# FFN weights split by the transfers that load them, and not by VectorE

## The chip, the cores and the metric

The kernel runs on one core of one Trainium2 chip. The metric is the device time of one execution in microseconds (us); the median of 3 runs of the kernel before is 906.88 us (905.92 to 911.09). A core has TensorE (PE: matrix products, with a row PEld for the loads of the stationary operand), VectorE (DVE), ScalarE (ACT), GpSimd (POOL) and SyncE (SP), each with an instruction stream that it takes in order. Transfers are issued from SP, ACT or POOL, run on 16 DMA engines that all of them share, and report their end through a semaphore.

## The reference

One layer of a decoder trunk is computed for 512 prompt positions and 8 sample rows (520 columns in all): a mixer sub-layer (window attention, a state-space branch "S5" and attention to a memory, gated and merged), and after it a channel sub-layer. Only that second part, the FFN, changes how it is fed:

```
def conv_ffn(h, lp, prev):
    a = h @ lp['w_ffn_gate']          # 1024 x 2816
    up = h @ lp['w_ffn_up']           # 1024 x 2816
    ...
    c = lp['conv_b'] + sum(w[j] * ext[:, j:j + T] for j in range(CONV_W))
    y = (jax.nn.gelu(c) * up) @ lp['w_ffn_down']   # 2816 x 1024
```

Products are wanted in float32 accuracy. TensorE is used in its faster float32r form, so each float32 operand is split into a rounded part "hi" and the rest "lo" = value - hi, and a product is taken as hi*hi + hi*lo + lo*hi: three matrix instructions in place of one.

## The kernel before

All weights lie in one tensor `in_w`, cut into 152 units of up to 8 blocks of 128x128 in the order of use (`UNITS`, line 43). A unit of 8 blocks is a tile of 128 partitions x 1024 float32, 512 KB. The last 68 units are the FFN's: 22 pairs "fg" (gate) and "fu" (up), and then 8 groups of three "dn" (down) units, of which the third has 6 blocks (384 KB). Before them stand 8 units "out" of the mixer's output projection.

Each unit takes three steps. `w_load` (line 323) issues the transfer into one of two raw tiles `wraw` from SP. `w_split` (line 335) has ACT round it into one of three tiles `whi`, and DVE subtract `whi` from `wraw` into one of three tiles `wlo`. Then `product` (line 449) issues the matrix products: 8 blocks x 2 halves of the columns x 3 = 48 instructions of 260 columns. The order is set in the code: `begin` (431) makes sure that unit i is split and units i+1 and i+2 are loaded, and in the middle of unit i `ahead` (441) splits i+1 and i+2 and loads i+3. By the time that `ahead` runs, i+1 is split and i+2 loaded, so what it really issues is the split of i+2 and after it the load of i+3.

In the FFN loop (line 1576) a pair also has, after "fg", DVE reading the result out of PSUM, a small copy on POOL, a convolution on ACT and DVE, an add and two more copies on POOL, a Gelu on ACT, and after "fu" a product, a rounding and a subtraction that make the hidden block's hi and lo. The "dn" loop (1616) has no work on POOL.

Up to the "out" units, smaller tasks (attention, S5, memory) are woven between the matrix products by a planner: `Clock` (line 79) books an estimated cost for every instruction, and `pump` (394) starts the next step of a task when the booked time says that it is ready. A transfer from POOL is booked in line 201 with one figure; the S5 task uses it where it writes a kernel matrix to a scratch tensor `kd` and reads it back (lines 1159 and 1164). In the FFN no such task is left and the planner moves nothing.

Lines 1547 and 1548 copy two caches from input to output (508 KB each) from POOL's queue. All instructions go through one helper, so the profile names line 226 for nearly all of them; tiles tell them apart.

Of the kernel before, what the change touches and what calls it, by code (L numbers as in the profile page):

```python
# [7 lines left out]
F32 = mybir.dt.float32  # L8
F32R = mybir.dt.float32r
I32 = mybir.dt.int32  # L10
AF = mybir.ActivationFunctionType
OP = mybir.AluOpType
# [3 lines left out]
P = 128  # L16
# [5 lines left out]
KB = DM // P  # L22
# [33 lines left out]
def stream_units():  # L56

    u = [("k", 0), ("v", 0)] + [("q", i) for i in range(4)]
    u += [(x[:-1], int(x[-1])) for x in SEQ0.split() if x != "vt"]
    u += [(x[:2], int(x[2])) for x in SEQ.split()]  # L60
    u += [("gB", i) for i in range(8)] + [("glu", i) for i in range(8)]
    u += [("out", i) for i in range(8)]
    for i in range(NFF):
        u += [("fg", i), ("fu", i)]
    for i in range(8):
        u += [("dn", (i, 0)), ("dn", (i, 1)), ("dn", (i, 2))]
    return u


UNITS = stream_units()  # L70


def unit_blocks(u):
    return 6 if u[0] == "dn" and u[1][1] == 2 else 8


UNIT_OFF = []
_o = 0
for _u in UNITS:
    UNIT_OFF.append(_o)  # L80
# [4 lines left out]
class Clock:  # L85
# [74 lines left out]
    def op(self, eng, name, a, k):  # L160
        outs = [a[0]] + ([k["accum_out"]] if "accum_out" in k else [])
        ins = [x for x in list(a[1:]) + list(k.values()) if hasattr(x, "ap") and x is not outs[-1]]
        shape = a[0].shape
        n = 1
        for d in shape[1:]:
            n *= d
        if eng == "sp":
            out, src = a
            n = 4
            for d in out.shape:  # L170
                n *= d
            t0 = max(self.t["sp"], self.deps(eng, [out], [src]))
            self.t["sp"] = t0 + 0.45
            self.t["hw"] = max(self.t["hw"], t0 + SP_A) + max(0.26, n / 360e3)
            self.note(eng, [out], [src], self.t["hw"] + SP_B)
            return
        if eng == "pe":
            if name == "transpose":
                c = 0.9e-3 * a[1].shape[0] + 0.003
            else:  # L180
                m, w = 1, 1
                for d in a[1].shape[1:]:
                    m *= d
                for d in a[2].shape[1:]:
                    w *= d
                c = 0.417e-3 * max(m, w) + 0.003 if a[1].dtype == F32R else 1.667e-3 * w * (1 if m > 64 else 0.5)
        elif eng == "act":
            c = 0.833e-3 * n + 0.094 * (1 + sum(hasattr(k.get(x), "ap") for x in ("bias", "scale", "accum_out")))
            if a[1].space == PSUM:
                c -= 0.043  # L190
        elif eng == "dve":
            if name == "tensor_reduce":
                n = 1
                for d in a[1].shape[1:]:
                    n *= d
            c = 0.07 + (6.3e-3 if name == "reciprocal" else 0.52e-3 if name == "tensor_copy" and a[1].space != PSUM
                        else 1.04e-3) * n
            if name == "tensor_tensor_reduce" or name == "scalar_tensor_tensor" and hasattr(a[2], "ap"):
                c += 0.06
        elif eng == "dma":  # L200
            c = 3.3
        else:
            c = {"tensor_tensor": 0.151 + 1.95e-3 * n, "tensor_scalar": 0.215, "memset": 0.035 + 0.833e-3 * n}.get(name, 0.12 + 3.3e-3 * n)
        q = "pool" if eng == "dma" else eng
        t0 = max(self.t[q], self.deps(eng, outs, ins))
        if eng == "pe" and t0 < COLD:
            c *= 2
        end = t0 + c
        self.t[q] = t0 + 1.1 if eng == "dma" else end
        self.note(eng, outs, ins, end)  # L210
        if eng != "dma":
            self.last = max(self.last, end + self.LAT)
        else:
            self.last_dma = end
# [26 lines left out]
HZ = 2.0  # L241
# [7 lines left out]
N_RAW = 2  # L249
# [7 lines left out]
def body(ctx, tc, I, O):  # L257
    nc = tc.nc
    clk = Clock()
    pe, act, dve, pool = [Eng(r, n, clk) for r, n in ((nc.tensor, "pe"), (nc.scalar, "act"), (nc.vector, "dve"),  # L260
                                                      (nc.gpsimd, "pool"))]
    sp = Eng(nc.sync, "sp", clk)
# [3 lines left out]
    wrw = ctx.enter_context(tc.tile_pool(name="wrw", bufs=N_RAW))  # L266
    wsp = ctx.enter_context(tc.tile_pool(name="wsp", bufs=3))
# [15 lines left out]
    def B_done(n=1):  # L283
        live["B"] -= n
# [36 lines left out]
    RAW, HI, LO = {}, {}, {}  # L321

    def w_load(i, parts=1):
        if i >= len(UNITS) or i in RAW:
            return
        n = unit_blocks(UNITS[i]) * P
        r = clk.tile(wrw.tile([P, KB * P], F32, name="wraw", tag="wraw"), "wraw", N_RAW)
        RAW[i] = r
        m = n // parts
        for c in range(parts):  # L330
            yield sp.dma_start(r[:, c * m:(c + 1) * m],
                               bass.AP(tensor=I["w"].tensor, offset=I["w"].offset + UNIT_OFF[i] + c * m,
                                       ap=[[n, P], [1, m]]))

    def w_split(i, part=None):

        if i >= len(UNITS) or (part is None and i in HI):
            return
        for _ in w_load(i):
            pass  # L340
        n = unit_blocks(UNITS[i]) * P
        if not part:
            HI[i] = clk.tile(wsp.tile([P, KB * P], F32R, name="whi", tag="whi"), "whi", 3)
            LO[i] = clk.tile(wsp.tile([P, KB * P], F32R, name="wlo", tag="wlo"), "wlo", 3)
        c = slice(0, n) if part is None else slice(part * n // 2, (part + 1) * n // 2)
        r = RAW[i]
        act.activation(HI[i][:, c], r[:, c], AF.Copy)
        dve.tensor_tensor(LO[i][:, c], r[:, c], HI[i].bitcast(F32)[:, c], op=OP.subtract)
# [9 lines left out]
    pos = [0]  # L358

    def run(l):  # L360
        clk.last = l.ready if l.eng else 0.0
        cur.append(l)
        try:
            r = next(l.gen)
            l.ready = clk.last
            l.eng, l.need, l.tiles = "pe", 1, 0
            if isinstance(r, tuple):
                r, l.tiles = r
            if isinstance(r, str):
                l.eng, l.need = r, 0  # L370
            elif isinstance(r, float):
                l.ready = max(l.ready, clk.last_dma) + r
            elif r is not None:
                l.need = abs(r)
                if r < 0:
                    l.eng = None
        except StopIteration:
            lanes.remove(l)
        cur.pop()

    ev = [EV]

    def unit_time(i):
        return {"mk": 2.65, "mv": 2.65, "sk": 0.85, "sv": 0.85}.get(UNITS[i][0], 5.3)

    def ready(l):

        if l.eng in ("dve", "act"):
            t = 0.0 if l.ready <= clk.t[l.eng] + MARG_Q else l.ready
        else:  # L390
            t = max(l.ready if l.eng else 0.0, clk.free("SD", 4, l.need))
        return max(t, clk.free("T2", N_T2, l.tiles))

    def pump(rem=0.0):

        while True:
            t = clk.t["pe"]
            lim = min(rem + ev[0], rem + sum(unit_time(j) for j in range(pos[0], min(max(HI) + 1, len(UNITS)))) - HZ)
            if clk.t["dve"] - t > min(BACK_D, lim) or clk.t["act"] - t > min(BACK_A, lim):
                return  # L400
            for l in lanes:
                if ready(l) <= t + MARG:
                    run(l)
                    break
            else:
                return
# [24 lines left out]
    def begin(name):  # L431
        i = pos[0]
        assert UNITS[i][0] == name, (UNITS[i], name)
        pos[0] += 1
        if i:
            w_split(i)
            load(i + 1)
            load(i + 2)
        return i
# [128 lines left out]
    sv = con.tile([P, 528], F32, name="sv")  # L568
    ap = sv[:, 0:288].rearrange("p (n r q) -> p n r q", n=9, r=2)
# [239 lines left out]
    for m in range(1, 4):  # L809
        i = begin("q")  # L810
# [699 lines left out]
    for m in range(8):  # L1510
        i = begin("glu")
# [23 lines left out]
    for m in range(8):  # L1535
        i = begin("out")
# [7 lines left out]
            dve.tensor_tensor(acc2, acc2, sq, op=OP.add)  # L1544


    pool.dma_start(O["sk"][:, :127 * 128], I["ckn"][:, 128:])
    pool.dma_start(O["sv"][:, :127 * 128], I["cvn"][:, 128:])
    B_done(2)
    hb = [B(F32R) for _ in range(5)]  # L1550
    hm = M(F32R)
# [24 lines left out]
    for ob in range(NFF):  # L1576
        i = begin("fg")
        if ob == 0:

            ps = product(i, range(8), blk(yh, yl), kouter=True, mid=norm2)  # L1580
            i = begin("fu")
# [7 lines left out]
        w = [cw[:, ob, j:j + 1] for j in range(3)]  # L1589
        c = T2()  # L1590
# [9 lines left out]
        if ob:  # L1600
            i = begin("fu")
# [14 lines left out]
    for m in range(7):  # L1616
        ps = out_tile()
        for c in range(3):
            i = begin("dn")
            n = unit_blocks(UNITS[i])  # L1620
# [209 lines left out]
```

## Time and profile before

| | |
|---|---|
| median of 3 runs | 906.88 us |
| the profiled execution | 907.0 us |
| its span, first to last instruction | 905.2 us |
| mean granted TensorE clock | 0.987 |
| PE busy | 883.5 us, 98% |
| DVE busy | 518.8 us, 57% |
| ACT busy | 344.8 us, 38% |
| POOL busy | 130.3 us, 14% |
| DMA | 97.83 MB, mean 108 GB/s |

A busy share is that of the whole span. Matrix instructions overlap each other, so the distance between their starts, and not their length, is the time that one of them takes. [...] POOL's own transfers are the profile's "software_dynamic" queue, SP's and ACT's are "hardware_dynamic".

### The profile page before, as it was taken

The page shows a single profiled execution, that of the slowest core. Times are in us where ns is not written, and L with a number is a line of the kernel's source. Part 1 is how long each engine was busy: PE and PEld are TensorE (multiplying, and loading weights), DVE is VectorE, ACT ScalarE, POOL GpSimd, SP SyncE. Part 2 cuts the span into 40 slices and gives each one's busy share as a digit, 9 for nine tenths or more (in the row PEclk, how much of TensorE's full clock was granted, in tenths as well). Part 3 has the DMA queues.
Part 4 walks back from the last instruction along what each step waited for, and adds up shares of the span by engine and source line. Part 5 has one row for each costly group of instructions (what it writes and reads, how often), then busy time and mean ns, then how long its engine had stood idle before and what let it go on. Part 6 is the DMA issues. An engine that isn't in the chain of part 4 may idle for free.

```text
span 905.2 us, 17660 instructions
## 1 busy us (share of the span) xinstructions
PE 883.5 (98%) x7417; PEld 854.0 (94%) x7417; DVE 518.8 (57%) x868; ACT 344.8 (38%) x596; POOL 130.3 (14%) x376
## 2 busy tenths in 40 slices
PE   8999999999899999999999999999999999999994
PEld 8998899998799899899999999999999999999993
DVE  6777768794465696023665665555555555232224
ACT  6376655544434322142333333333333333222231
POOL 7887110002000002100000010000110011000001
PEclk9999999999999999989999999999999999999997
DMA  7533482345424433524232323332222223223212
GB/s 253 171 93 102 128 183 71 117 134 135 89 79 151 120 97 115 137 70 171 91 98 89 103 81 95 93 94 93 94 92 93 88 90 97 94 88 105 89 42 94
DMA packets 38383, 97.83 MB, mean 108 GB/s; under 512 B 12464, under 2 KB 15968, under 8 KB 38032
## 3 DMA queue, kind: packets, MB, share of 16 engines
q1 hardware_dynamic: 35136, 89.53, 32.1%
q0 software_dynamic: 1936, 6.02, 3.0%
q8 instruction: 58, 0.95, 0.4%
q10 hardware_dynamic: 1232, 1.16, 0.4%
q14 instruction: 21, 0.17, 0.1%
HBM read 91.47 MB, written 6.26 MB: 108 GB/s over the span
## 4 chain that ended last, share of the span: by engine, by line
PE 86%; DMA 5%; DVE 4%; ACT 2%; issue 1%; POOL 1%; SPq 0%; DVEq 0%; ACTq 0%; POOLq 0%
PE mm L226 76%; PE SD L226 11%; DMA B<-kd 2%; DMA wraw<-in_w 2%; DVE B L226 1%; ACT T L226 1%; DVE T L226 1%; DMA out_fin<-B 1%; DMA B<-in_xT 1%; DVE wlo L226 1%; DMA kd<-B 1%; ACT whi L226 1%; ACT B L226 0%; POOL B L226 0%; DVE TN L226 0%
## 5 line engine op out<-in xcount | busy, mean ns | idle before, releaser
L226 PE MATMUL mm<-B,whi 128*128 128x260 f32 (+1 forms) x4128 | 761.5, 285 | 4.1 <-DVE B L226 2.4
L226 PEld LDWEIGHTS mm<-B,whi 128*128 128x128 f32 x4128 | 641.9, 189 | 12.4 <-issue 4.1
L226 PE MATMUL mm<-B,wlo 128*128 128x260 f32 (+1 forms) x2096 | 594.1, 283 | 1.1 <-DVE wlo L226 1.0
L226 PEld LDWEIGHTS mm<-B,wlo 128*128 128x128 f32 x2096 | 396.8, 189 | 1.9 <-DVE wlo L226 1.9
L226 DVE TENSOR_TENSOR wlo<-wraw,whi 128x1024 fp32r<-128x1024 f32 (+2 forms) x157 | 186.6, 1190 | 167.8 <-ACT whi L226 167.0
L226 ACT ACTIVATE whi<-wraw 128x1024 fp32r<-128x1024 f32 (+2 forms) x157 | 160.4, 1023 | 113.0 <-PE mm L226 71.2
L226 DVE SCALAR_TENSOR_TENSOR T<-T,sm,T 128x512 f32<-128x512 f32 x44 | 34.0, 772 | 25.8 <-ACT T L226 25.1
L226 ACT ACTIVATE T<-T,sm 128x520 f32<-128x520 f32 x22 | 18.1, 823 | 79.1 <-POOL T L226 79.1
L226 PE MATMUL SD<-B 128*64 128x72 f32 (+9 forms) x576 | 43.5, 248 | 0.8 <-DMA B<-kd 0.7
L226 DVE TENSOR_TENSOR B<-B 128x256 f32<-128x256 f32 (+11 forms) x78 | 36.3, 474 | 13.8 <-ACT B L226 12.4
L226 ACT ACTIVATE B<-T 128x520 fp32r<-128x520 f32 (+1 forms) x32 | 20.4, 638 | 55.0 <-DVE T L226 55.0
L226 POOL COPY T<-T 128x2 f32<-128x2 f32 x22 | 4.1, 184 | 255.1 <-DVE T L226 255.1
L226 PEld LDWEIGHTS SD<-B 128*64 128x64 f32 (+5 forms) x576 | 30.4, 126 | 10.9 <-issue 4.0
L226 ACT ACTIVATE B<-SD 128x256 fp32r<-128x256 f32 (+6 forms) x50 | 19.0, 406 | 53.5 <-PE SD L226 53.4
L226 DVE TENSOR_TENSOR T<-mm,rstd 128x520 f32<-128x520 f32 x22 | 15.4, 699 | 34.2 <-PE mm L226 31.1
L226 ACT ACTIVATE T<-B 128x520 f32<-128x520 f32 (+1 forms) x25 | 15.3, 611 | 39.8 <-DVE B L226 39.8
L226 ACT ACTIVATE T<-T 128x520 f32<-128x520 f32 (+2 forms) x26 | 16.0, 621 | 37.6 <-DVE T L226 35.9
L226 ACT ACTIVATE B<-B,sm 128x520 fp32r<-128x520 f32 (+1 forms) x23 | 16.7, 726 | 30.6 <-DVE B L226 27.3
L226 ACT ACTIVATE B<-mm 128x520 f32<-128x520 f32 x16 | 9.7, 605 | 47.3 <-PE mm L226 47.3
L226 DVE TENSOR_TENSOR B<-T,B 128x520 fp32r<-128x520 f32 (+1 forms) x30 | 19.2, 640 | 12.9 <-ACT B L226 12.7
L226 ACT ACTIVATE T<-T,TN 128x257 f32<-128x257 f32 (+3 forms) x48 | 21.8, 473 | 11.3 <-DVE TN L226 11.3
L226 POOL MEMSET T<- 128x2 f32 (+2 forms) x27 | 4.7, 175 | 147.4 <-DVE B L226 81.5
(156 smaller groups left out, 657.6 us busy)
## 6 DMA issues: line engine op xcount, KB each, us to landing
wraw<-in_w SPq DMA_DIRECT2D x144, 512.0 KB, 3.5
wraw<-in_w SPq DMA_DIRECT2D x8, 384.0 KB, 3.0
B<-in_xT SPq DMA_DIRECT2D x1, 2080.0 KB, 10.6
B<-kd POOLq DMA_DIRECT2D x16, 128.0 KB, 7.0
B<-in_xT SPq DMA_DIRECT2D x4, 260.0 KB, 6.3
B<-in_xT SPq DMA_DIRECT2D x2, 520.0 KB, 8.1
out_y<-B SPq DMA_DIRECT2D x4, 260.0 KB, 3.0
out_y<-B ACTq DMA_DIRECT2D x4, 260.0 KB, 3.2
```

What stands on the lines that cost most here:

```text
L226: return g(*a, **k)
```

## The change

For the FFN's 68 units the raw load from SP is gone. `w_load` issues a transfer from POOL whose destination is float32r, so that it writes the rounded hi part itself; the tiles used are five, two that were `wraw` and three `whi`. `w_split` has ACT write -hi into the `wlo` tile, and then POOL issues a second transfer of the same weights that adds them onto it: w + (-hi) = lo. DVE's subtraction is gone for these units, and each unit is read from memory twice. The planner books a POOL transfer at 5.0 in place of 3.3, and the two cache copies are issued from SP.

```diff
+FFN0 = UNITS.index(("fg", 0))
...
         elif eng == "dma":
-            c = 3.3
+            c = 5.0
...
     def w_load(i, parts=1):
         if i >= len(UNITS) or i in RAW:
             return
+        if i >= FFN0:
+
+            n = unit_blocks(UNITS[i]) * P
+            t = (clk.tile(wrw.tile([P, KB * P], F32R, name="wraw", tag="wraw"), "wraw", N_RAW) if i % 5 < 2 else
+                 clk.tile(wsp.tile([P, KB * P], F32R, name="whi", tag="whi"), "whi", 3))
+            RAW[i] = HI[i] = t
+            yield pool.dma_start(t[:, :n], w_dram(i))
+            return
...
+    def w_dram(i):
+        n = unit_blocks(UNITS[i]) * P
+        return bass.AP(tensor=I["w"].tensor, offset=I["w"].offset + UNIT_OFF[i], ap=[[n, P], [1, n]])
+
     def w_split(i, part=None):
 
-        if i >= len(UNITS) or (part is None and i in HI):
+        if i >= len(UNITS) or (part is None and i in LO):
             return
         for _ in w_load(i):
             pass
+        if i >= FFN0:
+
+            n = unit_blocks(UNITS[i]) * P
+            LO[i] = clk.tile(wsp.tile([P, KB * P], F32R, name="wlo", tag="wlo"), "wlo", 3)
+            act.activation(LO[i][:, :n], HI[i].bitcast(F32)[:, :n], AF.Copy, scale=-1.0)
+            pool.dma_start(LO[i][:, :n], w_dram(i), accum_op=OP.add)
+            return
...
-            lim = min(rem + ev[0], rem + sum(unit_time(j) for j in range(pos[0], min(max(HI) + 1, len(UNITS)))) - HZ)
+            lim = min(rem + ev[0], rem + sum(unit_time(j) for j in range(pos[0], min(max(LO) + 1, len(UNITS)))) - HZ)
...
-    pool.dma_start(O["sk"][:, :127 * 128], I["ckn"][:, 128:])
-    pool.dma_start(O["sv"][:, :127 * 128], I["cvn"][:, 128:])
+    sp.dma_start(O["sk"][:, :127 * 128], I["ckn"][:, 128:])
+    sp.dma_start(O["sv"][:, :127 * 128], I["cvn"][:, 128:])
```

How the instructions stand then is shown at three places. The first is POOL's stream in the middle of the FFN. T2 tiles are a pair's convolution tiles, M holds its small results. Before, POOL has only the small work of one pair after the other:

```order
L226 MEMSET T2_6650 128x2
L226 COPY T2_6650<-T2_6650 128x2
L226 TENSOR_TENSOR T2_6654<-T2_6654,M_5924 128x2x4
L226 COPY M_5924<-T2_6650 128x2
L226 COPY M_5924<-T2_6650 128x8
L226 MEMSET T2_6776 128x2
```

Now the four transfers of two units stand between the small work of two pairs (`wlo` is the adding transfer, `whi` or `wraw` the rounding one):

```order
L227 DMA wlo_7159<-in_w 128x1024
L227 DMA whi_7162<-in_w 128x1024
L227 DMA wlo_7216<-in_w 128x1024
L227 DMA whi_7219<-in_w 128x1024
L227 MEMSET T2_7257 128x2
L227 COPY T2_7257<-T2_7257 128x2
L227 TENSOR_TENSOR T2_7261<-T2_7261,M_5922 128x2x4
L227 COPY M_5922<-T2_7257 128x2
L227 COPY M_5922<-T2_7257 128x8
L227 DMA wlo_7283<-in_w 128x1024
L227 DMA wraw_7286<-in_w 128x1024
L227 DMA wlo_7340<-in_w 128x1024
```

In one in-order stream the adding transfer of unit j is followed by the rounding transfer of unit j+1, and that by the adding transfer of j+1.

The second place is ACT's stream there. Before, a pair has the convolution and the Gelu of "fg", the rounding of a unit, the rounding of the hidden block, and that of a second unit:

```order
L226 ACTIVATE T2_6402<-T2_6402 128x520
L226 ACTIVATE whi_6424<-wraw_6360 128x1024
L226 ACTIVATE B_5918<-T2_6402 128x520
L226 ACTIVATE whi_6482<-wraw_6428 128x1024
L226 ACTIVATE T2_6528<-T2_6524,sm_88 128x520
```

Now the two instructions on weights read the rounded tile and write the `wlo` tile, at the same places:

```order
L227 ACTIVATE T2_6393<-T2_6393 128x520
L227 ACTIVATE wlo_6415<-wraw_6351 128x1024
L227 ACTIVATE B_5916<-T2_6393 128x520
L227 ACTIVATE wlo_6472<-wraw_6418 128x1024
L227 ACTIVATE T2_6517<-T2_6513,sm_88 128x520
```

ACT keeps the number and the places of its instructions; what changes is what they wait for and who waits for them.

The third place is POOL's stream at the start of the FFN, around the last S5 transfers (`kd`), the cache copies and the small input `cfc`. Before:

```order
L226 DMA B<-kd 16x16x128 x8
L226 DMA out_fin<-B 128x288
L226 DMA out_sk<-in_ckn 8x16256
L226 DMA out_sv<-in_cvn 8x16256
L226 DMA M<-in_cfc 128x352
L226 COPY M<-M 128x22x8
L226 MEMSET T_6075 128x2
```

Now:

```order
L227 DMA B<-kd 16x16x128 x8
L227 DMA out_fin<-B 128x288
L227 DMA wraw<-in_w 128x1024
L227 DMA wlo<-in_w 128x1024
L227 DMA whi<-in_w 128x1024
L227 DMA wlo<-in_w 128x1024
L227 DMA whi<-in_w 128x1024
L227 DMA M<-in_cfc 128x352
L227 COPY M<-M 128x22x8
L227 DMA wlo<-in_w 128x1024
L227 DMA whi<-in_w 128x1024
```

The cache copies have left POOL, `cfc` stands behind the transfers of the first units, and a copy that needs `cfc` stands ahead of the adding transfer of the third unit.

## Rows read from the trace of the kernel before

**Rows 1.** The page: busy us (share), by engine.

```profile
PE 883.5 (98%) x7417; PEld 854.0 (94%) x7417; DVE 518.8 (57%) x868; ACT 344.8 (38%) x596; POOL 130.3 (14%) x376
```

**Rows 2.** The chain that ended last: start us, us, what.

```profile
392.59 120.24 PE mm L226 x1002
...
520.86 363.39 PE mm L226 x3039
```

**Rows 3.** By stretch: length, busy us (count) of PE, PEld, DVE, ACT, POOL; PEclk, DMA share, GB/s.

```profile
610.00:660.00 50.00, 50.00 (x422) 50.00 (x421) 29.12 (x36) 18.39 (x23) 5.51 (x24) 1.00 0.27 86
...
820.00:870.00 50.00, 50.00 (x419) 50.00 (x419) 14.43 (x15) 12.66 (x15) 0.00 (x0) 1.00 0.30 96
```

**Rows 4.** Tile wlo: engine, operation, count: ns min/median/max, first and last start, forms.

```profile
L226 DVE TENSOR_TENSOR wlo<-wraw,whi x157: 677/1225/1299, 5.6 to 877.4; 128x1024 fp32r<-128x1024 f32 x143, 128x768 fp32r<-128x768 f32 x8, 128x512 fp32r<-128x512 f32 x6
```

**Rows 5.** ACT's timeline, first and last FFN unit's rounding: start us, us, instruction, idle before.

```profile
499.72 1.04 ACT L226 ACTIVATE whi<-wraw 128x1024 fp32r<-128x1024 f32 x1
...
876.55 0.83 ACT L226 ACTIVATE whi<-wraw 128x768 fp32r<-128x768 f32 x1
```

**Rows 6.** PE's timeline at the end of the products.

```profile
891.38 0.60 PE L226 MATMUL SD<-T,ones 128*128 128x260 f32 x2
```

**Rows 7.** The timeline within one pair of the FFN, all engines.

```profile
563.19 0.70 DVE L226 TENSOR_TENSOR T<-mm,rstd 128x520 f32<-128x520 f32 x1 [1.60 <-PE mm L226]
...
563.95 0.18 POOL L226 COPY T<-T 128x2 f32<-128x2 f32 x1 [9.38 <-DVE T L226]
...
565.93 0.10 POOL L226 MEMSET T<- 128x2 f32 x1
...
570.73 1.05 ACT L226 ACTIVATE whi<-wraw 128x1024 fp32r<-128x1024 f32 x1
...
571.81 1.23 DVE L226 TENSOR_TENSOR wlo<-wraw,whi 128x1024 fp32r<-128x1024 f32 x1 [0.25 <-ACT whi L226]
```

**Rows 8.** DMA issues: transfer, queue, count, KB each, median us to landing.

```profile
wraw<-in_w SPq DMA_DIRECT2D x144, 512.0 KB, 3.5
wraw<-in_w SPq DMA_DIRECT2D x8, 384.0 KB, 3.0
...
out_mv<-B POOLq DMA_DIRECT2D x1, 512.0 KB, 9.1
...
B<-in_bm POOLq DMA_DIRECT2D x1, 256.0 KB, 3.0
...
B<-in_st POOLq DMA_DIRECT2D x1, 128.0 KB, 3.7
```

**Rows 9.** POOL's timeline where it issues transfers, and the copy behind `cfc`.

```profile
110.95 0.58 POOL L226 DMA_DIRECT2D B<-in_bm  x1
...
112.08 0.55 POOL L226 DMA_DIRECT2D B<-in_st  x1
...
119.64 0.58 POOL L226 DMA_DIRECT2D out_mk<-M  x1
120.22 0.55 POOL L226 DMA_DIRECT2D out_mv<-B  x1
...
377.37 0.33 POOL L226 COPY M<-M 128x176 f32<-128x176 f32 x1 [11.44 <-DMA M<-in_cfc]
```

**Rows 10.** DMA in 40 slices of 0.5 us: first of 560 to 580, then of 105 to 125.

```profile
GB/s 393 377 66 0 0 156 279 328 262 25 16 0 0 0 0 0 0 0 0 0 0 131 287 401 221 8 0 0 106 254 369 303 49 0 0 0 0 0 0 0
...
GB/s 0 0 0 0 0 123 238 369 295 25 24 42 0 0 123 205 344 401 180 88 2 0 82 115 344 330 311 143 86 86 121 107 111 116 100 127 123 132 220 296
```

**Rows 11.** PE's waits: for whom, us in total, times, longest.

```profile
PE mm L226 <- DVE B L226: 2.4, 3, 1.7
...
PE SD L226 <- DMA B<-kd: 0.7, 1, 0.7
```

**Rows 12.** By stretch, columns as in rows 3, in the S5 task's last step.

```profile
385.00:390.00 5.00, 5.00 (x32) 4.89 (x29) 1.23 (x1) 2.25 (x5) 0.00 (x0) 0.53 0.12 23
```

**Rows 13.** PE's timeline just before that stretch.

```profile
379.99 5.45 PE L226 MATMUL SD<-B 128*8 128x16 f32 x96
```

## The prediction

> **What bounds the kernel now.** I read the page's busy shares first, then the chain that ended last, then the FFN stretch by stretch, and only then single transfers. The shares say TensorE: 98% of the span, with VectorE at 57% [rows 1]. The chain says where there is nothing to win: from 392.59 us on it is matrix products almost without a break, and its longest piece is 3039 of them in 363.39 us from 520.86 [rows 2], that is 363.39 / 3039 = 119.6 ns each. A unit of 48 takes 5.74 us, and a pair 11.48 us. In the FFN PE is busy 50.00 us of 50.00 at a granted clock of 1.00, and the pace is the same where VectorE is busy 29.12 us of 50 (422 products) and where it is busy 14.43 (419) [rows 3]. So taking work off VectorE does not quicken the products: the reader is to see two stretches with half the VectorE work between them and one pace. VectorE's subtraction, 1225 ns for a unit [rows 4], is 68 x 1.2 = about 82 us of VectorE's time that nobody waits for; it is 1.23 us late in a pair in which VectorE also sits idle 1.60 us for PE [rows 7]. The gain of the change in the FFN is therefore bounded by nearly zero, and the question is whether the new way of supplying a unit keeps up with 5.74 us.
>
> **What the change puts in its place: a ring.** In the new order of POOL's stream the adding transfer of unit j is followed by the rounding transfer of j+1, and that by the adding transfer of j+1. The last one waits for ACT's -hi of j+1, which waits for the rounding transfer of j+1 to land. Nothing of unit j+2 can be issued meanwhile, because it stands behind in the same stream. So units follow each other at the time T of one turn: issue of adding j, issue and landing of rounding j+1, ACT's instruction, semaphores, issue of adding j+1. Before, SP issued a load ahead of time and nothing behind it depended on its landing; now two transfers of 512 KB and an ACT instruction lie end to end in each unit. If T is below 5.74 us PE does not notice. If it is above, the FFN runs at T.
>
> The terms of T:
> - ACT's instruction on 128x1024: 1.05 us [rows 7]. The hand-over to the next engine: 0.25 us, as DVE idles behind ACT now [rows 7]; POOL's would be much the same. Together 1.30.
> - From the issue of adding j to the landing of rounding j+1. An issue on POOL takes 0.55 to 0.58 us [rows 9]. The trace has no transfer that rounds or adds, so I bound the pair. Low end: the second does not feel the first and lands like SP's, 3.5 us [rows 8]: 0.56 + 3.5 = 4.06. High end: two transfers of 512 KB that POOL issued back to back at 119.64 and 120.22, where the second landed after 9.1 us [rows 8, 9]: 0.58 + 9.1 = 9.7; they write to memory beside SP's loads. Nearest: three loads into SBUF that POOL issued back to back, 640 KB in all, the third issued 1.13 us after the first and landed 3.7 us later [rows 8, 9]: 4.83 us. Their bytes moved within 3 us from 112.0 on, at up to 401 GB/s, and a 512 KB load of the FFN takes four to five slices of 0.5 us [rows 10]. Another 384 KB, at 0.5 us for 128 KB (the difference of 3.5 and 3.0 [rows 8]) 1.5 us or at the best slices' rate 1.0, makes 5.8 to 6.3. I take 6.0, near this row, since it has the same queue, direction and back-to-back issue. It counts rounding and adding as free in themselves.
>
> So T = 6.0 + 1.3 = 7.3 us, between 4.06 + 1.3 = 5.4 and 9.7 + 1.3 = 11.0. For the units of 384 KB each of the two transfers is 0.5 us shorter and ACT 0.2 [rows 5, 8], 1.2 us per unit.
>
> A rule that bears on the adding transfer is in the Trainium skill, "Collectives: The Full Stack", The bandwidth ceiling: an add in the DMA path is slower not for the arithmetic but because it reads two sources on the same ring, which halves its rate. No transfer here adds, so the trace can't agree or differ. By it the first transfer of the pair would move 1 MB, about 2 us more by the slices of [rows 10], T = 9.3; this is the case of the rival with a price of its own, below, which is worked out there from rows.
>
> **The rest of the change.** ACT has as many instructions as before at the same places; its -hi now waits for a transfer, and behind it stand the pair's convolution and Gelu. With the ring slower than PE these are not late: the unit whose result they need is itself two units behind. POOL's small work in a pair ends 2.8 us after PE is done with "fg" (563.19 to 565.93, [rows 7]) and lies while a rounding transfer is in flight, so it costs nothing; without that cover it would add up to 2.8 us to a pair. At the start the copy that needs `cfc` stands ahead of the third adding transfer, and the two cache copies (1 MB) run from SP on the same DMA engines as the first units: I put 3 us on both, once, between 0 and 12 (11.44 us is what that copy idled before, with the cache copies ahead of `cfc` [rows 9]). The five hi tiles and three `wlo` tiles are free in time: a `wlo` tile is needed again three turns later.
>
> The planner's 5.0 in place of 3.3 moves steps of the S5 task against the gates' products before 400 us. There PE waits 2.4 us for DVE's B tiles and 0.7 us for `kd` [rows 11], and after 5.45 us of 96 products of 16 columns [rows 13] a stretch of 5 us has a mean granted clock of 0.53, near the lower of its two levels (1.2 GHz of 2.4): 32 products [rows 12] where 42 fit at full clock [rows 3]. A few microseconds can go or come: -4 to +4, taken as 0.
>
> **The sum.** ACT's rounding for the first FFN unit starts at 499.72 [rows 5]; -hi ends and the adding transfer is issued at about 501.0. Behind it are 67 turns: 67 x 7.3 = 489, less 8 short units at 1.2, about 9: 480. The last adding transfer is issued at 981, lands some 3.5 us later (384 KB at 3.0 [rows 8] and 0.5 for the slower queue), and with the 3 us once at 987. When is it needed now? The products end at 891.38 [rows 6]; the last group runs as two halves of 66 products, 7.9 us each, and 0.4 for small ones, so it starts at 875.2 and needs its third unit 48 products later, at 881. 987 - 881 = 106 us late, and what follows shifts whole. The profiled execution took 907.0 us for a span of 905.2, 1.8 outside it, and stands 0.1 above the median of 906.88. 907 + 106 = **1013 us**.
>
> **The rivals.**
> - *The transfers do not queue on each other, and PE stays the bound: no change.* T = 5.4 if the rounding transfer lands in 3.5 us though the adding one is ahead of it. For it: the slices between loads in the FFN are empty, the DMA share there is 0.3 [rows 3, 10], and a single burst reaches 401 GB/s. Against it: both go through one queue and the trio of [rows 8, 9] did not land at 3.5. It decides at T of about 5.8: 3168 products of 119.6 ns and some 3 us of small ones before 891.38 put PE's start in the FFN at about 509.5, the first adding transfer would land at about 505, and a lead of 4.5 us lasts 67 turns that are 0.07 us too long. Then the time is 907 with the planner's -4 to +4: 903 to 911. The Trainium skill, "DMA: Bandwidth & Descriptors", Anatomy of one DMA — SWDGE (gpsimd) path, gives a POOL transfer 2.0 us and bytes / 436e3, 3.2 us here; the 256 KB load took 3.0 [rows 8] where it says 2.6. With that and no queueing T is an estimated 5.1.
> - *The planner's shift alone, better:* the FFN as before and the S5 waits gone: 903, at most 4 us faster.
> - *Adding or rounding has a price of its own:* the add reads its destination back, 512 KB more in the same queue, at 2 us: T = 9.3, so 67 x 2 = 134 us on top: 1147. With less, T = 8.2: 1013 + 60 = 1073. For it: three streams in place of two; against it: nothing in the trace, which has no such transfer.
> - *The change does not relieve what it says:* VectorE's 82 us go, but 14 to 29 us of 50 were busy, and PE waited for none of it. This holds in all cases and is why none is much faster.
>
> **How the numbers follow.** Likeliest, T between 5.9 and 8.2: 0.56; by 67 us per microsecond of T, from about 920 to 1073, around 1013. No change in the FFN (T under 5.8): 0.14 within half a per cent (some 4.5 us, about what a measurement of this kernel can tell from none) and 0.06 faster by the planner. Own price, T above 8.2: 0.24, half of it above 9.1. The range is 905 to 1130: it takes in the no-change case and the own price up to T = 9.0. Slower by over 0.5%: 0.80; same 0.14; faster 0.06.
>
> **What the changed profile would show.** If right: PE's busy share in the FFN under 90%, its idle time put down to DMA into `wlo`; the adding transfers on POOL spaced by T, each waiting for ACT's `wlo` and that for DMA into `whi` or `wraw`; landings of the rounding transfers near 5.4 us; the stretch from 520 us to the end longer by about 100 us and the stretch before 400 us within 4 us; DVE near 437 us busy. Wrong: PE at 50.00 of 50 in the FFN (T under 5.74), landings near 3.5, or a spacing set by POOL's small work or by ACT waiting for DVE instead. A granted clock that falls in the FFN's gaps would make it slower still: at 0.53 only 32 products fit in 5 us [rows 12]. I count none of that, as the stops of under 2 us in a unit are short beside its 5.74 us of products.

## The result and the profile after

The changed kernel takes 1092.67 us (median of 4 runs, 1091.23 to 1094.23) against 907.46 for the kernel before in the same runs (4 runs, 905.92 to 911.09): a ratio of 1.202, with an interval of 1.199 to 1.205. It is slower by 185 us; the prediction was 1013, slower by 106. The mechanism is the ring that the prediction described; its turn is 8.3 us in the mean of all 67, where the prediction's sum had 480 / 67 = 7.2.

The profiled execution took 1094.23 us for a span of 1092.5, 187.3 more than the span before. First the page's busy shares and its chain by engine, of the kernel after:

```profile
PE 955.0 (87%) x7417; PEld 911.9 (83%) x7417; DVE 439.3 (40%) x800; ACT 343.5 (31%) x594; POOL 231.4 (21%) x510
...
PE 42%; DMA 35%; ACT 8%; issue 6%; DVE 5%; POOL 3%; ACTq 0%; DVEq 0%; POOLq 0%
```

Against [rows 1], VectorE lost 79.5 us, where 82 were forecast, and TensorE went from 98% to 87% of a longer span. The chain that ended last was products almost throughout in [rows 2]; now 35% of it is DMA. The waits of POOL, ACT and PE in the kernel after (for whom, us in total, times, longest) say which transfers:

```profile
POOL wlo L227 <- ACT wlo L227: 390.3, 64, 9.6
...
ACT wlo L227 <- DMA whi<-in_w: 175.6, 35, 7.4
ACT wlo L227 <- DMA wraw<-in_w: 101.4, 21, 8.1
...
PE mm L227 <- DMA wlo<-in_w: 111.7, 57, 4.5
```

Read from the bottom: PE waits for the adding transfer, which POOL can't issue before ACT's -hi, which waits for the rounding transfer, which POOL issued behind the adding transfer of the unit before. POOL, ACT and the transfers wait for each other in a circle, and PE waits beside it; POOL and ACT are busy for 21% and 31% of the span. One turn of it, from the timeline of the kernel after (start us, us, instruction, idle before and its releaser):

```profile
598.85 0.89 POOL L227 DMA_DIRECT2D wlo<-in_w  x1 [5.46 <-ACT wlo L227]
599.45 0.86 POOL L227 DMA_DIRECT2D whi<-in_w  x1
...
604.39 0.39 PE L227 MATMUL mm<-B,wlo 128*128 128x260 f32 x1 [1.01 <-DMA wlo<-in_w]
...
605.67 1.06 ACT L227 ACTIVATE wlo<-whi 128x1024 fp32r<-128x1024 f32 x1 [6.59 <-issue]
...
607.03 0.87 POOL L227 DMA_DIRECT2D wlo<-in_w  x1 [6.73 <-ACT wlo L227]
```

From 598.85 to 607.03 is 8.18 us: 0.60 until the rounding transfer is issued, 6.22 until ACT starts on what it landed, 1.06 for ACT, 0.30 until POOL issues the next adding transfer. ACT's wait is put down to "issue" in this row, since the profile shows no event there; in 56 of ACT's 68 rows it names the rounding transfer (35 and 21, above), so I take the 6.22 us as its landing here too. All 68 adding transfers are in one row of the view by tile (count, ns min/median/max, first and last start in us), and the view of DMA issues (KB each, median us to landing) has both kinds:

```profile
L227 POOL DMA_DIRECT2D wlo<-in_w x68: 855/870/927, 505.4 to 1061.4; - x68
```

```profile
wraw<-in_w SPq DMA_DIRECT2D x84, 512.0 KB, 3.6
wlo<-in_w POOLq DMA_DIRECT2D x60, 512.0 KB, 5.5
whi<-in_w POOLq DMA_DIRECT2D x36, 512.0 KB, 6.2
wraw<-in_w POOLq DMA_DIRECT2D x24, 512.0 KB, 6.2
wlo<-in_w POOLq DMA_DIRECT2D x8, 384.0 KB, 4.8
```

(1061.4 - 505.4) / 67 = 8.30 us is the mean turn, short units included. By stretch (length, busy us and count of PE, PEld, DVE, ACT, POOL; PEclk, DMA share, GB/s), the two stretches of [rows 3] look like this after:

```profile
610.00:660.00 50.00, 40.07 (x285) 38.81 (x284) 12.61 (x18) 11.64 (x15) 11.65 (x26) 0.90 0.55 124
...
820.00:870.00 50.00, 40.29 (x288) 39.04 (x287) 12.42 (x18) 12.32 (x15) 12.69 (x27) 0.90 0.57 127
```

285 products in 50 us where 422 fitted: 285 / 48 = 5.9 units, 8.4 us each. The granted clock of 0.90 is a second loss on the face of it, and PE's timeline in one unit shows why next to nothing of it counts:

```profile
610.00 0.40 PE L227 MATMUL mm<-B,whi 128*128 128x260 f32 x2
612.52 0.39 PE L227 MATMUL mm<-B,wlo 128*128 128x260 f32 x1 [2.12 <-DMA wlo<-in_w]
...
613.46 0.42 PE L227 MATMUL mm<-B,wlo 128*128 128x260 f32 x1
613.68 0.64 PE L227 MATMUL mm<-B,whi 128*128 128x260 f32 x2
614.11 0.42 PE L227 MATMUL mm<-B,wlo 128*128 128x260 f32 x1
...
619.68 0.40 PE L227 MATMUL mm<-B,whi 128*128 128x260 f32 x2
620.88 0.39 PE L227 MATMUL mm<-B,wlo 128*128 128x260 f32 x1 [0.80 <-DMA wlo<-in_w]
```

After the wait of 2.12 us the products slow down: three take 0.65 us (613.46 to 614.11), and the granted clock from 613.5 to 616.5 is 0.50, the lower of its two levels (1.2 GHz of 2.4). Then they run at full clock. But PE still arrives at the next `wlo` 0.80 us too early. The slow products fill what would have been wait. So PE is "busy" 71.5 us more in the whole kernel (955.0 against 883.5) without work added, and 71.5 + 111.7 of waits for `wlo` + 4.1 of PE's other idle time come to the difference of 187.3. POOL, ACT and the transfers set the turn: 64 of the 68 adding transfers waited for ACT's -hi, and in none of the waits of the adding transfers or of ACT's -hi is PE named. Only behind the last landing does the clock count: from 1067.0 to 1070.5 us it is 0.52 with no wait left to fill, which is about 1.7 us.

What moved on the DMA engines, in slices of 0.5 us from 600 to 620 of the kernel after, whose pairs were issued at 598.85 and 607.03:

```profile
GB/s 25 41 131 172 221 188 221 270 418 393 16 33 0 0 0 0 0 131 33 164 180 197 213 238 434 401 107 0 0 0 0 0 0 115 16 66 213 164 246 213
```

The slices of a pair come to 1.06 MB. If the bytes move in the order of issue, the first 0.5 MB, the adding transfer, needs some seven slices, the last five at 131 to 221 GB/s; the rounding one then comes through in about three at up to 418. The plain loads of [rows 10] moved at up to 401.

### The profile page after: what moved, and what is told of

Read it like the earlier page. It is cut to its first block, busy times and chain, and to the rows that moved or that the text cites. A ratio compares the mean times of both kernels' runs of the same rounds, so it can differ in the third digit from the quotient of the medians.

```text
span 1092.5 us, 17587 instructions
## 1 busy us (share of the span) xinstructions
PE 955.0 (87%) x7417; PEld 911.9 (83%) x7417; DVE 439.3 (40%) x800; ACT 343.5 (31%) x594; POOL 231.4 (21%) x510
## 4 chain that ended last, share of the span: by engine, by line
PE 42%; DMA 35%; ACT 8%; issue 6%; DVE 5%; POOL 3%; ACTq 0%; DVEq 0%; POOLq 0%
PE mm L227 34%; DMA whi<-in_w 15%; DMA wraw<-in_w 12%; PE SD L227 9%; DMA wlo<-in_w 6%; ACT wlo L227 5%; DVE B L227 2%; POOL wlo L227 2%; DVE T L227 2%; ACT T L227 1%; DMA B<-kd 1%; DVE wlo L227 1%; ACT whi L227 1%; DMA M<-in_cfc 1%; ACT B L227 0%
## 5 line engine op out<-in xcount | busy, mean ns | idle before, releaser
L227 PE MATMUL mm<-B,wlo 128*128 128x260 f32 (+1 forms) x2096 | 625.2, 298 | 112.6 <-DMA wlo<-in_w 111.7
L227 PE MATMUL mm<-B,whi 128*128 128x260 f32 (+1 forms) x3312 | 642.8, 294 | 4.6 <-DVE T L227 2.5
L227 PEld LDWEIGHTS mm<-B,whi 128*128 128x128 f32 x3312 | 540.2, 198 | 13.0 <-issue 4.0
L227 PE MATMUL mm<-B,wraw 128*128 128x260 f32 x816 | 170.7, 307 | 0.1
L227 POOL DMA_DIRECT2D wlo<-in_w x68 | 59.5, 876 | 411.1 <-ACT wlo L227 390.3
L227 PEld LDWEIGHTS mm<-B,wraw 128*128 128x128 f32 x816 | 144.1, 214 | 0.5 <-DVE B L227 0.5
L227 DVE TENSOR_TENSOR wlo<-wraw,whi 128x1024 fp32r<-128x1024 f32 (+1 forms) x89 | 105.5, 1187 | 95.5 <-ACT whi L227 93.5
L227 ACT ACTIVATE wlo<-whi 128x1024 fp32r<-128x1024 f32 (+1 forms) x41 | 42.4, 1033 | 215.2 <-DMA whi<-in_w 175.6
L227 ACT ACTIVATE whi<-wraw 128x1024 fp32r<-128x1024 f32 (+1 forms) x89 | 90.8, 1023 | 46.5 <-PE mm L227 23.6
L227 POOL DMA_DIRECT2D whi<-in_w x41 | 34.7, 846 | 0.5 <-issue 0.5
```

Of the source, the lines that this page charges most:

```text
L227: return g(*a, **k)
```

## The experiments

Two theories stood after the result. A: the ring is the whole loss, and its turn is longer than forecast because adding has its own price in the transfer. B: the transfers as such (rounding, adding, POOL's queue) or the lower clock cost the time, ring or not. All times are compared with the kernel before, run on the same chip.

**e1, the add taken away.** The second transfer only rounds the weights into `wlo`; the subtraction is left out.

```
-            pool.dma_start(LO[i][:, :n], w_dram(i), accum_op=OP.add)
+            pool.dma_start(LO[i][:, :n], w_dram(i))
```

> The changed kernel with the second transfer of a unit writing the weights plainly over -hi, without the add (lo is then the rounded weight itself; that part of the computation is left out). The ring through POOL stays as it is. Theory (the ring sets the pace, and the add has a price of its own in the transfer: 512 KB in 2.9 us where a rounding transfer takes 1.3): a turn falls from 8.3 to about 6.8 us, adding transfers land after 4.0 in place of 5.5, time about 990 us (67 x 1.5 less than 1092). Rival (two POOL transfers back to back are slow as such, the add is free): a turn stays at 8.3, time 1092.

981.51 us (2 runs), ratio 1.081 [1.077, 1.085]. The ring is kept, only the add is gone; the view by tile and the issues of e1:

```profile
L227 POOL DMA_DIRECT2D wlo<-in_w x68: 537/540/570, 498.2 to 948.4; - x68
```

```profile
wlo<-in_w POOLq DMA_DIRECT2D x60, 512.0 KB, 3.9
whi<-in_w POOLq DMA_DIRECT2D x36, 512.0 KB, 4.7
```

The turn is (948.4 - 498.2) / 67 = 6.72 us. So the add costs 8.30 - 6.72 = 1.58 us in each turn, 106 us over 67. The pair without the add (both transfers still round) lands about 0.55 + 4.7 = 5.2 us after its first issue, 0.8 less than the 6.0 that I took; even so the ring alone costs 74 us, because 6.72 is still above 5.74.

**e2, the ring cut and everything else kept.** The loads of the next two units are issued ahead of the adding transfer.

```
         if i >= FFN0:
+            for j in (i + 1, i + 2):
+                for _ in w_load(j):
+                    pass
```

> The changed kernel with one more thing: before the adding transfer of unit i is issued, the rounding transfers of i+1 and i+2 are, so that the rounding one stands two units ahead of the adding one in POOL's stream. Same transfers, same bytes, same ACT work. Theory (the turn of the ring is latency, end to end): no -hi waits for a transfer any more, the two transfers of a unit move in about 5.2 us, under PE's 5.74, and PE is busy all the time again: 905 to 915 us. Rival (the two transfers of a unit, with the add's slow rate, don't go through in 5.74 us): the spacing stays above 6.5 us, 960 to 1092 us.

918.15 us (4 runs), ratio 1.010 [1.006, 1.013]. Of the 185 us, 175 are gone with the same transfers, the same bytes and the same ACT work, in another order. That decides for the ring of theory A, with some 10 us left over (e7 below); the price of adding is e1's. The stretches of e2:

```profile
610.00:660.00 50.00, 49.98 (x418) 49.61 (x417) 18.66 (x26) 17.60 (x22) 19.67 (x39) 1.00 0.82 179
...
820.00:870.00 50.00, 50.00 (x419) 50.00 (x418) 4.90 (x7) 13.02 (x16) 13.37 (x19) 1.00 0.87 182
```

The clock is back at 1.00 too: the fall of the kernel after came from the waits. The adding transfer lands later here (median 6.6 us) than in the ring (5.5), and does no harm. But the DMA share is 0.82 to 0.87, where it was 0.27 and 0.30 in [rows 3].

**e3, only the rounding transfer** in the kernel before (the code below shortens the names of tiles and addresses): hi from POOL's rounding transfer, the raw unit from SP, lo still from VectorE's subtraction. **e4, only the adding transfer:** hi from ACT as before, then -hi by ACT and an adding transfer in place of VectorE's subtraction.

```
 e3:
+        if i >= FFN0:
+            HI[i] = (a whi tile)
+            pool.dma_start(HI[i][:, :n], (unit i in in_w))
 ...
+            dve.tensor_tensor(LO[i][:, :n], RAW[i][:, :n], HI[i].bitcast(F32)[:, :n], op=OP.subtract)
 e4:
+        if i >= FFN0:
+            act.activation(LO[i][:, c], HI[i].bitcast(F32)[:, c], AF.Copy, scale=-1.0)
+            pool.dma_start(LO[i][:, c], (unit i in in_w), accum_op=OP.add)
+            return
```

> The kernel before with only the rounding moved: hi by a rounding transfer from POOL, the raw weights by SP as before, DVE subtracts as before. Two transfers of 512 KB a unit, on two queues, and no ring. Theory (ring): 903 to 912 us, rounding transfers land after 4 to 5 us and nobody waits. Rival (a rounding transfer is slow in itself, or 1 MB a unit is too much for the DMA engines): PE waits for DMA into whi or for DVE's wlo in every unit, over 930 us.

> The kernel before with only the subtraction moved: load from SP and rounding on ACT as before, then ACT writes -hi (one more ACT instruction of 1.05 us a unit) and POOL adds the weights onto it. No ring, since the load does not stand behind the add. Theory (ring): 905 to 920 us; the adding transfer lands 4.8 to 5.5 us after issue, which is about when PE wants it in the units behind fg, so some 0.4 us a pair may be lost. Rival (the adding transfer is too slow as such): PE waits for DMA into wlo in every unit, over 960 us.

e3: 920.51 us (2 runs), ratio 1.014 [1.011, 1.017]; the rounding transfer lands in 4.4 us. e4: 936.71 us (2 runs), ratio 1.032 [1.025, 1.038]; the adding one lands in 6.6. Neither has a ring, and neither comes near 1092, but both lie between the range of their theory and that of their rival, so neither expectation was met. The two stretches of e3, then of e4, and PE's longest wait in e4:

```profile
510.00:560.00 50.00, 44.84 (x358) 44.29 (x357) 26.67 (x45) 7.87 (x14) 11.34 (x26) 0.93 0.52 169
610.00:660.00 50.00, 50.00 (x422) 50.00 (x421) 28.59 (x35) 9.84 (x14) 12.75 (x34) 1.00 0.58 190
```

```profile
610.00:660.00 50.00, 48.71 (x400) 48.21 (x401) 18.01 (x25) 24.94 (x29) 14.37 (x29) 1.00 0.78 175
```

```profile
PE mm L227 <- DMA wlo<-in_w: 12.4, 17, 2.1
```

In e3 the steady FFN has its 422 products in 50 us, as before; what is lost is lost at the entry, before 560. There POOL issues `cfc` only at 515.39, behind rounding transfers that waited for PE; VectorE waits 6.90 us for `cfc` (to 524.02), PE waits 5.17 us for VectorE (to 529.29), and from 530 to 535 us PE makes 28 products at a granted clock of 0.58 where 44 fit at full clock. The waits of e3 between 500 and 540 us:

```profile
DVE M L227 <- DMA M<-in_cfc: 6.9, 1, 6.9
...
PE SD L227 <- DVE T L227: 5.2, 1, 5.2
```

In e4 PE waits 4.2 us at the same place. Besides, ACT of e4 is busy half of the time and PE waits for `wlo` 17 times: ACT's two passes for a unit stand behind each other, and 6.6 us of landing follow where VectorE needed 1.2.

**e8, e3 with its entry mended:** `cfc` and the cache copies are issued by SP, `cfc` first.

```
-    pool.dma_start(O["sk"][:, :127 * 128], I["ckn"][:, 128:])
-    pool.dma_start(O["sv"][:, :127 * 128], I["cvn"][:, 128:])
 ...
-    pool.dma_start(cm[:, 0:352], I["cfc"])
+    sp.dma_start(cm[:, 0:352], I["cfc"])
+    sp.dma_start(O["sk"][:, :127 * 128], I["ckn"][:, 128:])
+    sp.dma_start(O["sv"][:, :127 * 128], I["cvn"][:, 128:])
```

> The kernel with only the rounding moved to POOL transfers, and besides cfc and the cache copies issued from SP. Theory (rounding in the transfer costs nothing from unit to unit; the 13 us were lost once at the entry, in a wait of PE for VectorE, which waited for cfc): 905 to 911 us. Rival (the rounding transfer's 4.4 us landing or the doubled bytes cost something in each unit): 918 to 921.

910.7 us (10 runs), ratio 1.004 [1.001, 1.006]. Most of what e3 lost went with the late `cfc` (the run moves it and the cache copies together): PE's wait for VectorE at the entry is 1.3 us here. The rounding transfers themselves, 68 of them beside the plain loads, cost at most 0.6%, the upper end of the interval.

**e5, only the queue:** the FFN's plain loads issued by POOL in place of SP.

```
-            yield sp.dma_start(r[:, c * m:(c + 1) * m],
+            yield (pool if i >= FFN0 else sp).dma_start(r[:, c * m:(c + 1) * m],
```

> The kernel before with the FFN's raw loads issued from POOL in place of SP, plain, with nothing rounded or added on the way. It prices POOL's queue alone: 4.0 us to landing for 512 KB if it is 0.5 us slower than SP's 3.5, and 905 to 910 us. Rival (a POOL transfer of this size takes 5.5 us or more whatever it does): landing 5.5 to 6.2 us.

908.35 us (8 runs), ratio 0.999 [0.997, 1.001]: no difference. Its issues, POOL's plain transfers beside SP's:

```profile
wraw<-in_w SPq DMA_DIRECT2D x84, 512.0 KB, 3.6
wraw<-in_w POOLq DMA_DIRECT2D x60, 512.0 KB, 3.8
wraw<-in_w POOLq DMA_DIRECT2D x8, 384.0 KB, 3.3
```

These loads from SP are the mixer's; in the FFN of the kernel before SP's took 3.5 us, so POOL's queue makes 0.3 us of a landing. The 4.4 us of the rounding transfer in e3 show no price of rounding: SP's plain loads in the FFN of e3 (513 to 880 us) land after 4.3 us too, so with two streams of loads both are longer.

**e6, only the planner's 5.0 and the cache copies on SP.**

```
-            c = 3.3
+            c = 5.0
 ...
```

> The kernel before with the planner's 5.0 in place of 3.3 and the two cache copies on SP, the weights as before. In the changed kernel the first out units were reached 1.4 us earlier than before. Theory (that is the planner's doing): 905.5, 1.4 us faster. Rival (chance of one run): 907, no difference.

908.78 us (12 runs), ratio 1.000 [0.998, 1.002]. The gain that I expected of it isn't there, nor a loss. The kernel after reached the last part before the FFN 4.3 us later than the kernel before (474.25 against 469.91 at ACT's first instruction on the result of an "out" unit), not 1.4 us earlier, as the expectation has it. The profiled executions with 5.0 lie between 467.0 and 476.7 us at that place and those with 3.3 between 469.6 and 474.3, so this shift is not the planner's by any run here.

**e7, e2 with `cfc` mended as in e8.** The edit is that of e8 on top of e2.

> The kernel with the ring cut, and besides the small input cfc issued from SP ahead of the cache copies, in place of POOL behind the first units' transfers. Theory (with the ring cut, what is left over the kernel before is lost once, at the entry of the FFN, where VectorE and a POOL copy wait for cfc and the first adding transfers come late): 908 to 913 us, and PE's stretch from 500 to 540 us near 40 of 40 busy. Rival (it is lost in every unit to the adding transfer's slow landing of 6.6 us): 918, no difference.

919.96 us (4 runs), ratio 1.014 [1.010, 1.017]. This expectation failed: I had put e2's remaining loss on `cfc`, and it did not go. Where e2 loses its 13.9 us of span is read from one landmark, VectorE's first instruction on each pair's result, first and last pair, and PE's last product; before, then e2:

```profile
521.32 0.70 DVE L226 TENSOR_TENSOR T<-mm,rstd 128x520 f32<-128x520 f32 x1 [3.04 <-ACT rstd L226]
757.89 0.70 DVE L226 TENSOR_TENSOR T<-mm,rstd 128x520 f32<-128x520 f32 x1 [1.61 <-PE mm L226]
893.86 0.70 PE L226 MATMUL SD<-T,ones 128*128 128x260 f32 x2 [1.88 <-ACT T L226]
```

```profile
527.60 0.70 DVE L227 TENSOR_TENSOR T<-mm,rstd 128x520 f32<-128x520 f32 x1 [3.67 <-ACT rstd L227]
768.15 0.70 DVE L227 TENSOR_TENSOR T<-mm,rstd 128x520 f32<-128x520 f32 x1 [3.62 <-PE mm L227]
892.77 0.39 PE L227 MATMUL mm<-B,wlo 128*128 128x260 f32 x1 [2.01 <-DMA wlo<-in_w]
907.94 0.71 PE L227 MATMUL SD<-T,ones 128*128 128x260 f32 x2 [1.89 <-ACT T L227]
```

It loses 6.3 us before the first pair, 4.0 more over the next 21 pairs, and 3.8 behind the last one, and e7 5.6, 2.7 and 3.8. The piece at the end is plain: at 892.77 PE waits 2.01 us for the last unit, and the products behind it run at a granted clock of 0.68 to 895 and 0.80 to 900 us, about 1.7 us. ACT's rows just before, of e2:

```profile
885.50 0.64 ACT L227 ACTIVATE T<-B 128x520 f32<-128x520 f32 x1 [4.00 <-DVE B L227]
886.17 0.73 ACT L227 ACTIVATE B<-B,sm 128x520 f32<-128x520 f32 x1
886.81 0.83 ACT L227 ACTIVATE wlo<-whi 128x768 fp32r<-128x768 f32 x1
```

The -hi of the last unit stands behind work on the group's result, as the rounding did before [rows 5]. Before, VectorE finished the unit 0.96 us later; now an adding transfer of 4.8 us follows. The same longer way from ACT to `wlo` would explain four small waits over the 21 pairs (1.8 us in all), which I read and did not test; the rest of the 4.0 us there stays open. Of the 6.3 us at the entry, e2 was 1.5 late at the place named under e6 already, one wait for `wlo` is 2.97 (at 513.99), and from 515 to 520 us PE makes 36 products at a granted clock of 0.69 where the kernel before makes 45, about 1.1; some 0.7 stays open. In e7 3.4 of the 5.6 us are that late start.

**e9, one more term in the ring:** ACT computes -hi twice.

```
             act.activation(LO[i][:, :n], HI[i].bitcast(F32)[:, :n], AF.Copy, scale=-1.0)
+            act.activation(LO[i][:, :n], HI[i].bitcast(F32)[:, :n], AF.Copy, scale=-1.0)
```

> The changed kernel with ACT writing -hi twice, one more instruction of 1.05 us between the rounding transfer and the adding one. ACT has room (344 us busy of 1092). Theory (all terms of a turn lie end to end): a turn of 8.3 becomes 9.3, time 1092 + 67 x 1.0 = 1160 us. Rival (the two transfers' throughput sets the turn, ACT's work is hidden under it): 1092 to 1100.

1166.63 us (2 runs), ratio 1.285 [1.280, 1.290]. ACT has 68 more instructions of 1.05 us and is still idle most of the time (35% busy), yet the kernel is 74 us slower than the changed one. The row by tile of e9:

```profile
L227 POOL DMA_DIRECT2D wlo<-in_w x68: 857/870/925, 509.0 to 1136.6; - x68
```

The turn is (1136.6 - 509.0) / 67 = 9.37, longer by 1.07: one ACT instruction whole. The terms of the turn lie end to end, as theory A has it. A larger ACT time would have been hidden if PE or the transfers' rate had set the pace.

## Why the prediction was right in kind and short by 80 us

- *What bounds the kernel before, and what the change relieves.* Right: VectorE's 79.5 us less brought nothing; with its work unchanged (e3, e8) or removed (e2, e7) the steady FFN runs at 410 to 422 products in 50 us. (The 1.23 us that it calls late are the length of the subtraction [rows 7].)
- *The ring.* Right, in order and in who waits for whom; e2 takes it away, and 175 of the 185 us with it, and e9 lengthens each turn by the one instruction that was added.
- *ACT and the hand-over, 1.3 us.* Right: 1.06 + 0.30.
- *The pair, 6.0 us.* This is the term that was mis-sized. It was taken from three plain loads and counted "rounding and adding as free in themselves". The pair of the kernel after takes 0.60 + 6.22 = 6.8. e1 splits the error: a pair without the add takes 5.2, so 0.8 too much was taken for it, and adding, which was put at nothing, takes 1.58. By luck the two errors work against each other: with 5.2 and a free add the sum would have come to some 960 us. The rival "adding or rounding has a price of its own", with T above 8.2 and 1073 to 1147 us, is the case that came, by its adding half; rounding shows no price of its own (e5, e8).
- *The rule of the Trainium skill* ("Collectives: The Full Stack", The bandwidth ceiling, told there for the add of a collective) that an add in the path reads two sources on one ring and so halves its rate: the slices of the kernel after agree roughly, 131 to 221 GB/s for the adding half of a pair against up to 418 for the rounding half; in e1, without the add, the first half of a pair climbs to 344 GB/s within four slices (602 to 604 us). That a second read is the reason is not shown here. The Trainium skill gives no price in microseconds there; measured it is 1.58 us on 512 KB. The prediction had estimated 2 us by it and set that on top of a pair that was 0.8 too long.
- *The sum.* Predicted: first issue 501.0, 480 us of turns, last issue 981. Measured: 505.4, 556.0 and 1061.4. Turns make +76, which is 1.13 each: 0.8 for the pair, 0.1 for ACT and hand-over, the rest slow turns (up to 9.56 us; the rounding's landing lies between 5.4 and 7.3, and in two turns the hand-over took 1.13 and 1.35) and short units that save less than 1.2 us. The first issue makes +4.4. The last landing takes 4.6 where 3.5 was set (+1.1), the 3 us booked once for `cfc` and the cache copies don't show in the turns (8.49, 8.31 and 8.12 for the first three), and the way from the last landing to PE's last products took 2 more, most of it the lower clock there. Together some 80.
- *The planner at 0.* Not contradicted: e6 shows none.
- *The clock.* "I count none of that" was right as to the time, but for 1.7 us at the end, and wrong as to the reason: behind stops of some 2 us the clock did fall, to 0.90 over the FFN, but the slow products filled what would have been wait.
- *What was to be seen.* PE at 80% of the FFN (under 90% was forecast), its waits put down to `wlo`, VectorE at 439 (437), all as written; the spacing of 7.3 and the landing of 5.4 were not (8.30 and 6.2), and the part before the FFN came 4.3 us late where a shift within 4 was forecast.

The same bytes also cost more of the DMA engines, by the DMA share. A load took 0.27 to 0.30 x 5.74 = 1.5 to 1.7 us of them per unit before [rows 3]. In e3, with two loads, it is 0.58 x 5.74 = 3.3 and in the kernel after 0.56 x 8.3 = 4.6. So an adding transfer takes about 3 us of the 16 engines where a plain or rounding one takes 1.6. The pages of the two profiles agree: POOL's queue has 31.0% of 1092.5 us in the kernel after and 25.0% of 978.2 in e1, 94 us apart, 1.4 for each of 68 adding transfers. Had the ring been absent, 4.6 of 5.74 would still have fitted, which e2 shows with its 0.82 to 0.87.

## What to carry to other kernels

When a load ahead of time is replaced by a transfer that depends on a computed tile, look at what stands behind it in its issuing engine's stream: if the next unit's independent load does, the supply has turned into a ring, and its period is the sum of all latencies in it, however idle each engine looks. The cure is order, not speed: issuing the independent loads two units ahead gave back 175 of 185 us. And a transfer that does arithmetic gets a price of its own in the sum, from the side of the bounds that hurts, even where no row shows one.

## What the runs showed of the hardware

- Median landing of 512 KB from HBM to SBUF: 3.5 us issued by SP (FFN of the kernel before) and 3.8 plain from POOL (e5). With a second stream of loads beside it: 4.3 plain from SP and 4.4 rounding from POOL (e3), 6.6 adding (e4, e2). In the back-to-back pair of the ring the adding one lands in 5.5 and the rounding one behind it in 6.2; without the add 3.9 and 4.7. The adding transfer of the last unit, 384 KB alone, took 4.6 us.
- POOL's issue instruction lasts 0.54 us in e1 and 0.87 for an adding transfer in every kernel that has one; a rounding transfer's lasts 0.85 in the kernel after, right behind an adding one, and 0.58 in e2. In the kernel after the next one still starts 0.55 to 0.60 later.
- TensorE's products ran at the lower clock level (granted clock 0.50) from 613.5 to 616.5, just after the wait of 2.12 us, and at full pace (granted clock 1.00) after the waits of 1.01 us (604.39) and 0.80 (620.88). Where PE itself set the pace, the fall cost time: in e3, behind its wait of 5.17 us, 28 products in 5 us at 0.58, where 44 fit.
